# The MLP's first product as a seven-product step over channel pairs, with its result kept in DRAM

## The chip, the cores and the metric

The kernel runs on one core of a Trainium2 chip. A core has five engines that run their own instruction streams side by side and meet at semaphores: TensorE (PE in the profile, with its weight loads as PEld), VectorE (DVE), ScalarE (ACT), GpSimd (POOL) and SyncE (SP), which here issues nearly all DMA transfers, in the order of its stream. The time is that of the device for one execution, in microseconds (us); the median of several executions counts, and less is better.

## The reference, cut to what matters

The program computes two transformer-like blocks on 1024 tokens of width 1024: one with a recurrent mixer and a mixture of experts, then one with attention and an MLP. Only the end of the second block is touched:

```python
def second_block(x, c, ...):                     # cut to its last lines
    x = x + g_m * y                              # y: the attention's output product
    h = rms_norm_2(x, norm_mlp[i]) * (1 + sc_f) + sh_f
    x = x + g_f * (jnp.square(jax.nn.relu(h @ w_mlp_in[i])) @ w_mlp_out[i])
    return x                                     # h: 1024 x 1024, w_mlp_in: 1024 x 4096, w_mlp_out: 4096 x 1024
```

All is float32. The kernel splits each operand of a product into a high and a low part (both in the type fp32r) and adds three products: high by high, low by high, high by low.

## The kernel before, in words

The attention's output product (tiles "op", weights owh and owl, operand oyh and oyl) is made for eight tiles x2 of 128 tokens each. For the last four, tt = 4 to 7, the loop "for tt in range(4, 8)" issues per tile the loads of x (line 2152), a multiplication by fg on POOL (2153), the products, and the sum on DVE (1276, 2154). Between them stand the norms: net.norm_tiles makes xn from x2 (ACT line 820, DVE 84 to 97 and 823), and to_hT transposes xn on PE (834) and writes the operand of the MLP, h3h and h3l, split (ACT 836 and 841, DVE 839 and 842). There are 8 channel blocks k of 128, and two token halves of 512: half 0 is in place before the MLP starts, half 1 is made by last_half() in its midst.

The MLP (_mlp) runs over eight chunks c of 512 inner rows. phase_a(c) makes the first product: for each of four blocks u of 128 inner rows it loads 128 columns of w_mlp_in (line 74, tile ur), splits them into uh and ul (helper split: ACT line 66, DVE line 67), and for both token halves accumulates 8 x 3 matmuls of 128x128 by 512 columns in PSUM (proj_unit, mm3, lines 854 to 856, tile pj). Then ACT takes the relu (1592), DVE squares (1593), and a split writes mh and ml. phase_b(c) makes the second product: it loads and splits four blocks of w_mlp_out (w2h, w2l), and for each of eight token tiles accumulates 2 x 12 matmuls (tile mo); DVE multiplies by the gate (1633) and adds to x2 (1634). Chunk after chunk, the two phases alternate; in the last chunk x2 goes out (1636). In names such as pj<-h3h,uh the moving operand stands first and the stationary one second.

No list sets the order here: a scheduler orders each engine's stream, by the program's order and by when it reckons the operands to be there. Pools are stacks in SBUF, one growing from the left and one from the right (side=R).

Of the kernel before, what the change touches and what calls it, by code (L numbers as in the profile page):

```python
# [13 lines left out]
ALU = mybir.AluOpType  # L14
# [1561 lines left out]
def _mlp(self, wp, bp, ps, hT, w1, w2, x2, gate_row, out, last_half, first):

    nc = self.nc
    v = nc.vector
    gb = bp.tile([P, D], F32, name="mgb")  # L1580
    nc.sync.dma_start(gb, gate_row.to_broadcast([P, D]))
    NF = 8

    def phase_a(c):
        mids = [[bp.tile([P, S], F32R, name=n, bufs=5) for n in ("mh", "ml")] for u in range(4)]

        def piece(w, u, half):
            mh, ml = mids[u]
            sl = slice(half * 512, (half + 1) * 512)
            pt = self.proj_unit(ps, w, hT, half)  # L1590
            r = bp.tile([P, 512], F32, name="mr", bufs=2)
            nc.scalar.activation(r, pt, AF.Relu)  # L1592
            v.tensor_mul(r, r, pt)  # L1593
            self.split(mh[:, sl], ml[:, sl], r)

        def weight(u):
            f0 = c * 512 + u * P
            return self.wunit(wp, w1[:, f0:f0 + P])

        if c == 0:  # L1600
            for half in range(2):
                if half:
                    pools.extend(last_half())
                for u in range(4):
                    piece(first if (u, half) == (0, 0) else weight(u), u, half)
        else:
            for u in range(4):
                w = weight(u)
                for half in range(2):
                    piece(w, u, half)  # L1610
        return mids

    pools = []

    def phase_b(c, mids):
        W = []
        w2p = pools[0]
        for u in range(4):
            f0 = c * 512 + u * P
            raw = wp.tile([P, KC, P], F32, name="ur", bufs=2).rearrange("p k n -> p (k n)")  # L1620
            W.append(self.load_split(w2p, lambda r: [(r, w2[f0:f0 + P, :])], [P, D], "w2", 4, raw=raw))
        for tt in range(TT):
            sl = slice(tt * P, (tt + 1) * P)
            pts = [pools[1].tile([P, 512], F32, name="mo", bufs=4) for _ in range(2)]
            for u in range(4):
                for n in range(2):
                    cc = slice(n * 512, (n + 1) * 512)
                    self.mm3(pts[n], mids[u][0][:, sl], mids[u][1][:, sl], W[u][0][:, cc], W[u][1][:, cc],
                             u == 0, u == 3)
            for n in range(2):  # L1630
                cc = slice(n * 512, (n + 1) * 512)
                t = bp.tile([P, 512], F32, name="mt", bufs=1)
                v.tensor_mul(t, pts[n], gb[:, cc])  # L1633
                v.tensor_add(x2[tt][:, cc], x2[tt][:, cc], t)
            if c == NF - 1:
                nc.sync.dma_start(out[sl, :], x2[tt])
# [21 lines left out]
def program(net, ctx, I, out, dbg):  # L1658
# [35 lines left out]
    def each(t):  # L1694
        return [t[:, k:k + 1] for k in range(KC)]
# [442 lines left out]
        cf.close()  # L2138
    with ExitStack() as cx:
        xa = net.pool(cx, "x2a", side=R)  # L2140
        x2 = [xa.tile([P, D], F32, name=f"x2_{tt}") for tt in range(4)]
        co = ExitStack()
        ops = net.pool(co, "op_ps", space=PSUM, side="right")
        fg = net.pool(co, "fg2", side=R).tile([P, D], F32, name="fg2")
        nc.sync.dma_start(fg, final_g)
        op = OutProj(net, co, oTd, I["fox_w_out_2"][0], modd[1][2:3, :], ops, 2, x2, R, rd)

        def units(tts):
            for tt, n in tts:
# [51 lines left out]
        def norms(half):
            xns = []
            for i in range(4):
                tt = half * 4 + i
                xn = np_.tile([P, D], F32, name="xn", bufs=4)
                net.norm_tiles(np_, x2[tt], xn, rs[:, 0, tt:tt + 1], xn)
                xns.append(xn)
            return net.to_hT(np_, nps, 4 * half, xns, each(sc3), each(sh3), hT)
# [16 lines left out]
        wp = net.pool(cx, "ml_w", side=R)
        ps = net.pool(cx, "ml_ps", space=PSUM, side="right")

        def last_half():
            norms(1)
            cn.close()  # L2230
            return net.pool(cx, "ml_w2"), net.pool(cx, "ml_ps2", space=PSUM)

        net.mlp(wp, bp, ps, hT, I["w_mlp_in_2"][0], I["w_mlp_out_2"][0], x2, modd[1][5:6, :], out, last_half, first)
# [20 lines left out]
```

## Time and profile before

| what | us |
|---|---|
| median of 3 runs | 2637.94 |
| lowest and highest run | 2636.4 and 2642.43 |
| the profiled execution: its own time | 2636.1 |
| the profiled execution: its span | 2634.3 |

The span is what the profiler shows, from the first to the last instruction; the time holds a little more. Shares and stretches below are of the profiled execution. Starts are counted in us from the span's start. Matmul durations overlap, since one enters the array while the one before leaves it: a matmul of 512 columns is shown with about 0.39 us though the next starts after 0.23 us. The rate is therefore read from starts, or from a count of weight loads in a stretch.

### The profile page before, as it was taken

Reading aid. Unit: us, or ns where it says so; the run is one execution under the profiler, and the core shown is the slowest. Engines: PE = TensorE matmul, PEld = TensorE weight load, DVE = VectorE, ACT = ScalarE, POOL = GpSimd, SP = SyncE. Lnnn points to the kernel's source line nnn. Section 1 sums busy time; section 2 is a strip of 40 time slices with the busy share of each in tenths; the row PEclk is TensorE's granted clock in tenths of the full one; section 3 lists DMA queues with packets and bytes.
Section 4 is the critical chain, followed back from the end, with each engine's and each line's share of the span. In section 5 each row is a group of like instructions: output and inputs, shape, how many; then the busy total and the mean of one; then the engine's idle time right before and its main releaser. Section 6 shows DMA issues by size and latency. Waiting matters only on the chain.

```text
span 2634.3 us, 34681 instructions
## 1 busy us (share of the span) xinstructions
PE 2430.7 (92%) x11981; PEld 1950.9 (74%) x11981; DVE 1889.7 (72%) x3472; ACT 1335.8 (51%) x2435; POOL 424.9 (16%) x451
## 2 busy tenths in 40 slices
PE   6899989949999999986999999989999999999999
PEld 5677667737776666544898999977778888888887
DVE  7879886887979888986777887776654454444444
ACT  5556563246867767775677777763342122112210
POOL 2212110042314343531000000114100000000000
PEclk9999998969999999997999999999999999999999
DMA  8455564869999999983012111136141022112201
GB/s 268 126 148 177 160 219 146 272 246 299 369 346 367 338 358 326 367 310 114 28 49 49 48 47 47 36 90 189 46 122 48 17 64 64 35 30 64 64 28 69
DMA packets 243886, 407.86 MB, mean 155 GB/s; under 512 B 20432, under 2 KB 100164, under 8 KB 243708
## 3 DMA queue, kind: packets, MB, share of 16 engines
q1 hardware_dynamic: 235556, 386.70, 43.9%
q0 software_dynamic: 8032, 18.89, 3.2%
q8 instruction: 95, 1.56, 0.2%
q14 instruction: 83, 0.68, 0.1%
q10 hardware_dynamic: 120, 0.03, 0.0%
HBM read 376.74 MB, written 35.86 MB: 157 GB/s over the span
## 4 chain that ended last, share of the span: by engine, by line
PE 71%; DVE 14%; ACT 6%; DMA 4%; issue 4%; POOL 1%; SPq 0%; DVEq 0%; ACTq 0%; POOLq 0%
PE pj L854 8%; PE pj L855 8%; PE pj L856 8%; PE mo L854 5%; PE mo L856 5%; PE mo L855 5%; PE po L1513 2%; DVE wl L67 2%; PE op L856 2%; PE op L855 2%; PE op L854 2%; DVE aacc L782 2%; PE pT L1524 2%; PE pt L534 1%; PE pu L500 1%
## 5 line engine op out<-in xcount | busy, mean ns | idle before, releaser
L1592 ACT ACTIVATE mr<-pj 128x512 f32<-128x512 f32 x64 | 38.3, 598 | 497.2 <-PE pj L856 497.2
L67 DVE TENSOR_TENSOR wl<-wr,wh 128x1024 fp32r<-128x1024 f32 x210 | 249.8, 1229 | 28.8 <-ACT wh L66 27.7
L66 ACT ACTIVATE wh<-wr 128x1024 fp32r<-128x1024 f32 x216 | 220.5, 1054 | 86.7 <-PE po L464 30.9
L67 DVE TENSOR_TENSOR wl<-x,wh 128x1024 fp32r<-128x1024 f32 x164 | 192.4, 1217 | 26.3 <-ACT wh L66 25.6
L1633 DVE TENSOR_TENSOR mt<-mo,mgb 128x512 f32<-128x512 f32 x128 | 88.5, 692 | 163.6 <-PE mo L856 157.0
L854 PE MATMUL mo<-w2h,mh 128*128 128x512 f32 x512 | 202.5, 396 | 0.0
L855 PE MATMUL mo<-w2h,ml 128*128 128x512 f32 x512 | 202.5, 396 | 0.0
L856 PE MATMUL mo<-w2l,mh 128*128 128x512 f32 x512 | 202.5, 396 | 0.0
L854 PE MATMUL pj<-h3h,uh 128*128 128x512 f32 x504 | 198.7, 394 | 2.4 <-issue 2.4
L855 PE MATMUL pj<-h3h,ul 128*128 128x512 f32 x504 | 199.1, 395 | 0.9 <-DVE ul L67 0.9
L856 PE MATMUL pj<-h3l,uh 128*128 128x512 f32 x504 | 198.3, 394 | 0.0
L66 ACT ACTIVATE wh<-x 128x1024 fp32r<-128x1024 f32 x168 | 172.7, 1058 | 41.7 <-issue 9.1
L591 POOL DMA_INDIRECT x1d<-y,gidx x56 | 152.7, 2727 | 238.7 <-DMA x1d<-y,gidx 102.2
L854 PE MATMUL pj<-xh,h2h 128*128 128x384 f32 (+1 forms) x512 | 190.3, 372 | 0.8 <-DVE V L1433 0.7
L855 PE MATMUL pj<-xh,h2l 128*128 128x384 f32 (+1 forms) x512 | 176.0, 344 | 0.0
L856 PE MATMUL pj<-xl,h2h 128*128 128x384 f32 (+1 forms) x512 | 174.7, 342 | 0.0
L1593 DVE TENSOR_TENSOR mr<-mr,pj 128x512 f32<-128x512 f32 x64 | 44.0, 687 | 161.3 <-ACT mr L1592 161.3
L782 DVE SCALAR_TENSOR_TENSOR aacc<-aw,cs,aacc 128x512 f32<-128x512 f32 x160 | 131.1, 822 | 26.0 <-DMA aw<-in_w_ada 13.8
L67 DVE TENSOR_TENSOR pl<-pT,ph 128x512 fp32r<-128x512 f32 (+1 forms) x160 | 100.8, 634 | 25.0 <-ACT ph L66 21.5
L1501 ACT ACTIVATE Sx<-Sx,mx 128x128 f32<-128x128 f32 (+7 forms) x128 | 99.0, 773 | 38.3 <-DVE mx L1496 37.8
L856 PEld LDWEIGHTS mo<-w2l,mh 128*128 128x128 f32 x512 | 96.2, 188 | 23.3
L854 PEld LDWEIGHTS mo<-w2h,mh 128*128 128x128 f32 x512 | 96.2, 188 | 23.3
(525 smaller groups left out, 6591.5 us busy)
## 6 DMA issues: line engine op xcount, KB each, us to landing
wr<-in_w_expert_down SPq DMA_DIRECT2D x43, 1024.0 KB
wr<-in_w_expert_up SPq DMA_DIRECT2D x33, 1024.0 KB
x<-in_w_expert_gate SPq DMA_DIRECT2D x32, 1024.0 KB
wr<-in_w_expert_gate SPq DMA_DIRECT2D x32, 1024.0 KB
x<-in_w_expert_up SPq DMA_DIRECT2D x31, 1024.0 KB
aw<-in_w_ada SPq DMA_DIRECT2D x48, 512.0 KB
x<-in_w_expert_down SPq DMA_DIRECT2D x21, 1024.0 KB
aw<-in_ada_w SPq DMA_DIRECT2D x40, 512.0 KB
```

What stands on the lines that cost most here:

```text
L66: self.nc.scalar.activation(hi, src, AF.Copy)
L67: (v or self.nc.vector).tensor_sub(lo, src, hi.bitcast(F32))
L591: nc.gpsimd.indirect_dma_start(out=m.xd, out_offset=bass.IndirectOffsetOnAxis(ap=gi[0:r], axis=0), in_=y[o:o + r], in_offset=None, bounds_ ...
L782: nc.vector.scalar_tensor_tensor(acc, t[:, r, :], ccol[:, q:q + 1], acc, op0=ALU.mult, op1=ALU.add)
L854: nc.tensor.matmul(pt, sh, mh, start=first, stop=False)
L855: nc.tensor.matmul(pt, sl, mh, start=False, stop=False)
L856: nc.tensor.matmul(pt, sh, ml, start=False, stop=last)
L1501: nc.scalar.activation(Sx[:, 0:wd], Sx[:, 0:wd], AF.Exp, bias=mx[:, m - 1:m], scale=-1.0, accum_out=sm[:, q:q + 1])
L1513: nc.tensor.matmul(oc, vv, tiles[n][2 + t][:, at[r]:at[r] + 256], start=(kb + r == 0 and t == 0), stop=(kb + r == 2 * j + 1 and t == 1))
L1524: nc.tensor.transpose(pp[:, at[r] + q * P:at[r] + (q + 1) * P], Pj[q][:, (kb + r) * P:(kb + r + 1) * P], net.ident)
L1593: v.tensor_mul(r, r, pt)
L1633: v.tensor_mul(t, pts[n], gb[:, cc])
```

## The change

Two blocks of 128 inner rows, n's pair, are made together, and the contraction over 1024 channels is cut into two halves of 512 (k = 0 to 3 and 4 to 7). With the two token halves this gives a 2 by 2 by 2 block product, which a Strassen step (in Winograd's form) does with seven products of 4 x 3 matmuls instead of eight. The class Mlp holds the numbers o = 0 to 6 of the products. Their moving operands hc0 to hc6 are made once: hc0 and hc1 are the two channel halves of token half 0, hc2 to hc6 are token half 1 and sums and differences, made by half1(kk) in four steps between the first products. The stationary operands wc are made per pair from raw columns of w_mlp_in (rings of six raw tiles wr and four wc): prep adds or subtracts on POOL (lines 1648, 1650, 1651, 1656), then splits. step(g) calls prep(g + 3), issues product g's 12 matmuls and sums the results on DVE (1687 to 1702). inner takes relu and square in one DVE instruction (1707) and stores 512 columns to DRAM (rD). All 16 pairs are finished before the second product starts; that one loads the inner rows back ("m") with w_mlp_out ("w"), splits both (item) into the space of hc0 to hc6, and runs as before (block). The first four tiles of x2 go to DRAM and come back at g = 20, since half1 uses their space. PE's stream in the MLP is now fixed by hand.

```diff
-    for c in range(NF):
-        phase_b(c, phase_a(c))
+class Mlp:
+    NP = 16
+    LOOK = 3
...
+        duo = lambda a, os: [(n, o) for o in os for n in (a, a + 1)]
+        self.order = [(0, 0), (0, 1), (1, 0), (1, 1), (2, 0), (2, 1), (3, 0), (3, 1)]
+        self.todo = [("p", n) for n in range(4)]
+        for a in range(0, self.NP, 2):
+            self.order += duo(a, (3, 2, 4, 5, 6) if a < 4 else (0, 1, 3, 2, 4, 5, 6))
+            self.todo += [(k, a + i) for k in ("fg" if a else "gf") for i in range(2)]
+        self.todo += [(k, c, u) for c in range(8) for u in range(4) for k in "mw"]
...
+    def prep(self, g):
...
+        if o == 0:
+            src = A11
+        elif o == 1:
+            src = A12
+        elif o == 3:
+            src = self.S1[n] = self.pool.tile([P, 512], F32, name="hTt", bufs=2).rearrange("p (k n) -> p k n", k=4)
+            gp.tensor_add(src, A21, A22)
+        elif o == 2:
+            gp.tensor_sub(A21, A11, A21)
+            gp.tensor_sub(A11, self.S1.pop(n), A11)
+            src = A11
+        elif o == 4:
+            src = A21
+        elif o == 5:
+            gp.tensor_sub(A12, A12, A11)
+            src = A12
         else:
...
+            src = A22
+        wc = self.wc[g] = self.early.pop(0) if self.early else self.wp.tile([P, 2, 4, P], F32R, name="wc", bufs=4)
+        self.net.split(wc[:, 0], wc[:, 1], src)
...
+    def step(self, g):
...
+        self.prep(g + self.LOOK)
...
+        wc, h = self.wc.pop(g), self.hc[o]
+        for k in range(4):
+            net.mm3(pt, wc[:, 0, k, :], wc[:, 1, k, :], h[:, k, 0, :], h[:, k, 1, :], k == 0, k == 3)
+        if o == 0:
+            s = self.s[n] = self.wp.tile([P, 512], F32, name="s", bufs=4)
+            nc.scalar.activation(s, pt, AF.Copy)
...
+        elif o == 4:
+            s = self.s[n]
+            u = self.u[n] = self.wp.tile([P, 512], F32, name="c", bufs=4)
+            r = self.wp.tile([P, 512], F32, name="c", bufs=4)
+            v.tensor_add(u, s, pt)
+            z = self.Z.pop(n)
+            v.tensor_add(r, u, z)
+            v.tensor_add(s, s, z)
+            self.inner(r, n, 1, 1)
...
+    def inner(self, s, n, i, m):
+
+        self.net.nc.vector.scalar_tensor_tensor(s, s, 0.0, s, op0=ALU.max, op1=ALU.mult)
+        self.net.nc.sync.dma_start(self.rD[n][i][:, HALF[m]], s)
...
+        flat = [self.hc[o].rearrange("p k a n -> p (k a n)") for o in (0, 1, 3, 2, 4, 5, 6)]
+        self.slots = [t[:, i * 2048:(i + 1) * 2048].rearrange("p (a n) -> p a n", a=2) for t in flat for i in range(2)]
+        self.items = [(k, c, u) for c in range(8) for u in range(4) for k in "mw"]
...
+        hc = {o: xb.tile([P, 4, 2, 512], F32R, name=f"hc{o}") for o in range(2)}
...
+        hp = net.pool(cx, "hT3b", side=R)
+        for o in range(2, 7):
+            hc[o] = hp.tile([P, 4, 2, 512], F32R, name=f"hc{o}")
...
+            v.tensor_sub(T, t12, h[0][:, 0, :].bitcast(F32))
+            v.tensor_sub(T, T, h[0][:, 1, :].bitcast(F32))
+            net.split(h[3][:, 0, :], h[3][:, 1, :], T)
+            nc.gpsimd.tensor_sub(t12, t22, t12)
+            nc.gpsimd.tensor_sub(T, t22, T)
+            net.split(h[5][:, 0, :], h[5][:, 1, :], t22)
+            net.split(h[2][:, 0, :], h[2][:, 1, :], T)
+            net.split(h[4][:, 0, :], h[4][:, 1, :], t12)
+            nc.gpsimd.tensor_sub(t22, h[1][:, 0, :].bitcast(F32), T)
+            v.tensor_add(t22, t22, h[1][:, 1, :].bitcast(F32))
+            net.split(h[6][:, 0, :], h[6][:, 1, :], t22)
+
+        with tc.manual_schedule(engines={mybir.EngineType.PE}):
+            for g in range(len(mlp.order)):
+                if g in range(2, 6):
+                    half1(g - 2)
...
+                mlp.step(g)
```

Two places show how the streams move. The first is POOL at the start of the MLP. Before, its last work is the multiplication of x2's tiles 6 and 7 by fg, and the branch at the program's end follows:

```order
L2153 TENSOR_TENSOR x2_4_19574<-x2_4_19574,fg2_18831 128x1024 [waits DMAHW5_49,DVE_49]
L2153 TENSOR_TENSOR x2_5_19575<-x2_5_19575,fg2_18831 128x1024 [waits DMAHW6_49,DVE_49]
L2153 TENSOR_TENSOR x2_6_19576<-x2_6_19576,fg2_18831 128x1024 [waits DMAHW7_49,DVE_49]
L2153 TENSOR_TENSOR x2_7_19577<-x2_7_19577,fg2_18831 128x1024 [waits DMAHW0_49,DVE_49]
L1653 UNCONDITIONAL_BRANCH
```

Now, from half1's last step on (2363, 2364 and 2368 are its three POOL lines; wr_20354 and wr_20356 are the raw tiles "g" of pairs 0 and 1, wr_20358 and wr_20360 their "f", hTt_20370 and hTt_20392 the sums for product 3):

```order
L2363 TENSOR_TENSOR x2a_18854<-x2a_18854 128x512 [waits DVE_49]
L1648 TENSOR_TENSOR hTt_20370<-wr_20354 128x512 [waits DMAHW1_49,DVE_49,Pool_49]
L1650 TENSOR_TENSOR wr_20354<-wr_20358,wr_20354 128x512 [waits DMAHW5_49,DMAHW7_49,DMAHW3_49,Pool_49]
L1651 TENSOR_TENSOR wr_20358<-hTt_20370,wr_20358 128x512 [waits PE_49,Pool_49]
L1656 TENSOR_TENSOR wr_20358<-wr_20358 128x512 [waits Pool_49]
L2364 TENSOR_TENSOR hTt_20337<-x2a_18854,hTt_20337 128x512 [waits DVE_49]
L2368 TENSOR_TENSOR x2a_18854<-hc1_19613,hTt_20337 128x512 [waits Pool_49]
L1648 TENSOR_TENSOR hTt_20392<-wr_20356 128x512 [waits DMAHW4_49,DVE_49]
L1650 TENSOR_TENSOR wr_20356<-wr_20360,wr_20356 128x512 [waits DMAHW7_49,Pool_49]
L1651 TENSOR_TENSOR wr_20360<-hTt_20392,wr_20360 128x512 [waits PE_49,Pool_49]
```

Four POOL instructions for pair 0 now stand between the first and the second of half1's last step, and pair 1's sum behind both; nine more of half1 stand ahead.

The second place is DVE at the same time. Before, while half 1 of h3 is made (h3l1_2 to h3l1_5 are its low parts, mr the inner rows, ml their low parts, ul a weight's low part):

```order
L1593 TENSOR_TENSOR mr_20211<-mr_20211,pj_20186 128x512 [waits Activation_49]
L842 TENSOR_TENSOR h3l1_2_20048<-hTt_20295,h3h1_2_20047 128x512 [waits Activation_49]
L67 TENSOR_TENSOR ml_20077<-mr_20211,mh_20076 128x512 [waits Activation_49]
L839 CAST h3h1_3_20049<-hTt_20304 128x512 [waits Activation_49]
L842 TENSOR_TENSOR h3l1_3_20050<-hTt_20304,h3h1_3_20049 128x512 [waits DVE_49]
L842 TENSOR_TENSOR h3l1_4_20052<-hTt_20313,h3h1_4_20051 128x512 [waits Activation_49]
L839 CAST h3h1_5_20053<-hTt_20322 128x512 [waits Activation_49]
L842 TENSOR_TENSOR h3l1_5_20054<-hTt_20322,h3h1_5_20053 128x512 [waits DVE_49]
L67 TENSOR_TENSOR ul_20391<-ur_20388,uh_20390 128x1024 [waits DMAHW7_49,PE_49,Activation_49]
```

Now, the end of the same work (wc_20372, wc_20394, wc_20414 and wc_20436 are the stationary operands of steps 8 to 11, hTt_20337 and x2a the temporaries of half1's last step):

```order
L67 TENSOR_TENSOR hc3_20133<-hTt_20337,hc3_20133 128x512 [waits Activation_49]
L67 TENSOR_TENSOR wc_20372<-hTt_20370,wc_20372 128x512 [waits PE_49,Pool_49]
L1687 TENSOR_TENSOR c_20388<-s_20323,X_20375 128x512 [waits PE_49]
L67 TENSOR_TENSOR hc2_20132<-hTt_20337,hc2_20132 128x512 [waits Activation_49]
L2369 TENSOR_TENSOR x2a_18854<-x2a_18854,hc1_19613 128x512 [waits Pool_49]
L1707 SCALAR_TENSOR_TENSOR c_20388<-c_20388 128x512 [waits DVE_49]
L67 TENSOR_TENSOR wc_20394<-hTt_20392,wc_20394 128x512 [waits Activation_49]
L67 TENSOR_TENSOR hc6_20136<-x2a_18854,hc6_20136 128x512 [waits Activation_49]
L67 TENSOR_TENSOR wc_20414<-wr_20358,wc_20414 128x512 [waits DMAHW5_49,PE_49]
L1687 TENSOR_TENSOR c_20430<-s_20410,X_20417 128x512 [waits PE_49]
L67 TENSOR_TENSOR wc_20436<-wr_20360,wc_20436 128x512 [waits DMAHW7_49,Activation_49]
```

From half1's first subtraction (line 2360) to the last of these rows DVE now has 43 instructions of 128x512, of which three read PSUM (line 1687) and 40 read two operands from SBUF.

## Rows read from the trace of the kernel before

**Rows 1.** The page: busy time by engine, and the chain by engine.

```profile
PE 2430.7 (92%) x11981; PEld 1950.9 (74%) x11981; DVE 1889.7 (72%) x3472; ACT 1335.8 (51%) x2435; POOL 424.9 (16%) x451
...
PE 71%; DVE 14%; ACT 6%; DMA 4%; issue 4%; POOL 1%; SPq 0%; DVEq 0%; ACTq 0%; POOLq 0%
```

**Rows 2.** Stretches of the MLP: length, busy by engine (count), clock, DMA.

```profile
core 0: us, PE busy (x) PEld busy (x) DVE busy (x) ACT busy (x) POOL busy (x), PEclk, DMA share, GB/s
1959.90:2004.70 44.80, 44.80 (x193) 36.07 (x192) 24.99 (x35) 4.26 (x5) 0.00 (x0) 1.00 0.17 49
2004.70:2048.97 44.27, 44.27 (x194) 36.05 (x192) 19.95 (x25) 14.95 (x21) 0.00 (x0) 1.00 0.27 84
...
2628.20:2634.30 6.10, 0.13 (x1) 0.00 (x0) 2.23 (x4) 0.00 (x0) 0.00 (x0) 0.90 0.21 86
```

**Rows 3.** Two pieces of one first-product chunk: half 0, then half 1.

```profile
2004.70:2010.30 5.60, 5.60 (x25) 4.51 (x24) 2.27 (x4) 0.00 (x0) 0.00 (x0) 1.00 0.00 0
2010.30:2015.77 5.47, 5.47 (x26) 4.51 (x24) 1.38 (x2) 1.23 (x2) 0.00 (x0) 1.00 0.01 3
```

**Rows 4.** Matmuls by tile: ns min/median/max, first and last start.

```profile
L854 PE MATMUL mo<-w2h,mh x512: 395/396/397, 1959.9 to 2627.5; 128*128 128x512 f32 x171
...
L854 PE MATMUL pj<-h3h,uh x504: 389/395/628, 1915.0 to 2582.7; 128*128 128x512 f32 x168
...
L854 PE MATMUL pj<-h1h,uh x256: 387/389/793, 44.2 to 354.2; 128*128 128x512 f32 x128
```

**Rows 5.** Groups of lines, the attention's output product, 1880 to 1905.

```profile
L854 PE MATMUL op<-owh,oyh 128*128 128x512 f32 x38 | 14.8, 389 | 0.0
```

**Rows 6.** The MLP's start, by stretches.

```profile
1905.50:1912.50 7.00, 6.78 (x33) 5.26 (x31) 2.98 (x8) 1.64 (x5) 0.00 (x0) 1.00 0.52 153
1912.50:1915.00 2.50, 0.10 (x1) 0.01 (x1) 0.73 (x2) 1.65 (x3) 0.00 (x0) 1.00 0.82 202
1915.00:1920.00 5.00, 4.24 (x11) 3.18 (x12) 4.71 (x6) 3.51 (x5) 0.00 (x0) 0.66 0.42 118
```

**Rows 7.** The chain of waits there: start, length, what.

```profile
1907.63 6.21 DMA ur<-in_w_mlp_in
```

**Rows 8.** ACT in order of time, same place.

```profile
1907.28 1.06 ACT L820 ACTIVATE xn<-x 128x1024 f32<-128x1024 f32 x1 [9.07 <-DVE x L2154]
...
1914.83 0.61 ACT L66 ACTIVATE mh<-mr 128x512 fp32r<-128x512 f32 x1
...
1916.51 0.76 ACT L836 ACTIVATE hTt<-hTp,cols,sc 128x512 f32<-128x512 f32 x1
```

**Rows 9.** POOL in order of time, 1777 to 1790.

```profile
1778.01 1.69 POOL L1260 TENSOR_TENSOR x<-x,rb 128x512 f32<-128x512 f32 x1 [1.68 <-DMA rb<-rd]
1782.23 1.28 POOL L1260 TENSOR_TENSOR x<-x,rb 128x512 f32<-128x512 f32 x1 [2.53 <-DMA rb<-rd]
...
1786.90 1.63 POOL L1260 TENSOR_TENSOR x<-x,rb 128x512 f32<-128x512 f32 x1
```

**Rows 10.** DVE in order of time, beside those POOL instructions.

```profile
1777.89 0.69 DVE L67 TENSOR_TENSOR oyl<-x,oyh 128x512 fp32r<-128x512 f32 x1
1778.49 1.75 DVE L67 TENSOR_TENSOR owl<-x,owh 128x512 fp32r<-128x512 f32 x1
...
1786.69 0.68 DVE L67 TENSOR_TENSOR owl<-x,owh 128x512 fp32r<-128x512 f32 x1
1787.29 0.68 DVE L67 TENSOR_TENSOR pl<-pT,ph 128x512 fp32r<-128x512 f32 x1
1787.89 0.68 DVE L1496 CUSTOM_DVE_ANT_0 Sx<-Fb,pS 128x512 f32<-128x512 f32 x1
```

**Rows 11.** POOL's groups with shapes apart, whole span.

```profile
L2153 POOL TENSOR_TENSOR x<-x,fg 128x1024 f32<-128x1024 f32 x8 | 19.4, 2441 | 23.3 <-DVE rs_t L96 15.0 <-DVE x L2154 3.9 <-DMA x<-x1d 3.8
L1260 POOL TENSOR_TENSOR x<-x,rb 128x512 f32<-128x512 f32 x14 | 19.0, 1360 | 26.2 <-DMA rb<-rd 24.9 <-DVE x L2154 1.3
```

**Rows 12.** DVE's groups with shapes apart, 1950 to 2600.

```profile
L1634 DVE TENSOR_TENSOR x<-x,mt 128x512 f32<-128x512 f32 x116 | 80.2, 691 | 4.0
...
L67 DVE TENSOR_TENSOR w2l<-ur,w2h 128x1024 fp32r<-128x1024 f32 x32 | 39.2, 1224 | 10.5 <-ACT w2h L66 10.4
```

More of the change, by code (lines that the diff above doesn't have):

```diff
@@ L1573, in attend @@
         return front, back, gates
[L1576 to L1605, printed above, removed]
-        else:
[L1607 to L1621, printed above, removed]
@@ L1622, in phase_b @@
         for tt in range(TT):
             sl = slice(tt * P, (tt + 1) * P)
-            pts = [pools[1].tile([P, 512], F32, name="mo", bufs=4) for _ in range(2)]
+            pts = [self.px.tile([P, 512], F32, name="X", bufs=6) for _ in range(2)]
             for u in range(4):
+                m, w = self.op["m", c, u], self.op["w", c, u]
                 for n in range(2):
-                    cc = slice(n * 512, (n + 1) * 512)
-                    self.mm3(pts[n], mids[u][0][:, sl], mids[u][1][:, sl], W[u][0][:, cc], W[u][1][:, cc],
-                             u == 0, u == 3)
+                    net.mm3(pts[n], m[:, 0, sl], m[:, 1, sl], w[:, 0, HALF[n]], w[:, 1, HALF[n]], u == 0, u == 3)
+                if tt == TT - 1 and u == 0:
+                    for _ in range(2):
+                        self.item()
@@ L1630, in phase_b @@
             for n in range(2):
[L1631 to L1636, printed above, removed]
-    for c in range(NF):
-        phase_b(c, phase_a(c))
-Net.mlp = _mlp
+                cc = HALF[n]
+                t = self.wp.tile([P, 512], F32, name="s", bufs=4)
@@ L1645 @@
+                v.tensor_mul(t, pts[n], self.gb[:, cc])
+                v.tensor_add(self.x2[tt][:, cc], self.x2[tt][:, cc], t)
+            if c == 7:
+                nc.sync.dma_start(self.out[sl, :], self.x2[tt])
+            if tt < 6 and self.at < 8 * c + 14:
+                self.item()
 _INS = ["x", "c", "ada_w", "ada_b", "norm1_g", "w_in", "conv_w", "conv_b", "w_q", "w_k", "b_igate", "b_fgate",
@@ L1679, in program @@
     x1d = scratch("x1d", [S, D])
+    x2d = scratch("x2d", [512, D])
+    rD = [[scratch(f"rD{n}_{i}", [P, S]) for i in range(2)] for n in range(Mlp.NP)]
     oTd = [scratch(f"oTd{i}", [D, 512]) for i in range(2)]
@@ L2140, in program @@
         xa = net.pool(cx, "x2a", side=R)
-        x2 = [xa.tile([P, D], F32, name=f"x2_{tt}") for tt in range(4)]
+        x2a = xa.tile([P, 4, D], F32, name="x2a")
+        x2 = [x2a[:, tt, :] for tt in range(4)]
         co = ExitStack()
@@ L2194, in program, with norm @@
         x2 += [xb.tile([P, D], F32, name=f"x2_{tt}") for tt in range(4, 8)]
+        hc = {o: xb.tile([P, 4, 2, 512], F32R, name=f"hc{o}") for o in range(2)}
         hT = HT()
-        hT.alloc(0, xb, "h3")
+        hT.t[0] = [tuple(hc[k // 4][:, k % 4, a, :] for a in range(2)) for k in range(KC)]
+        np_ = net.pool(cx, "n4")
         cn = ExitStack()
-        np_ = net.pool(cn, "n4")
         nps = net.pool(cn, "n4_ps", space=PSUM)
[L2201 to L2208, printed above, removed]
+        mlp = Mlp(net, np_, hc, I["w_mlp_in_2"][0], I["w_mlp_out_2"][0], rD)
+        mlp.early = []
+        def norm(tt, t):
+            xn = t.rearrange("p k n -> p (k n)")
+            net.norm_tiles(np_, x2[tt], xn, rs[:, 0, tt:tt + 1], xn)
+            return xn
         for k in range(KC):
@@ L2225, in program @@
[L2225 to L2233, printed above, removed]
+                xns = [mlp.slot(("x", i)) for i in range(4)]
+                last = net.to_hT(np_, nps, 0, [norm(i, xns[i]) for i in range(4)], each(sc3), each(sh3), hT)
@@ new lines, in program @@
+                mlp.loads(2)
+                for i in range(4):
+                    mlp.done(("x", i))
+                xns = [mlp.slot(("x", i)) for i in range(4, 8)]
+            xns[tt - 4] = norm(tt, xns[tt - 4])
+        co.close()
+        mlp.wp = net.pool(cx, "ml_w", side=R)
+        for g in range(Mlp.LOOK):
+            mlp.prep(g)
+        hp = net.pool(cx, "hT3b", side=R)
+        for o in range(2, 7):
+            hc[o] = hp.tile([P, 4, 2, 512], F32R, name=f"hc{o}")
+        mlp.px = net.pool(cx, "ml_ps", space=PSUM, side=R)
@@ new lines, in program, with half1 @@
+        tmp = x2a.rearrange("p t (a n) -> p (t a) n", a=2)
+        def half1(kk):
+            t12, t22 = tmp[:, kk, :], tmp[:, 4 + kk, :]
+            for k, t in ((kk, t12), (kk + 4, t22)):
+                pt = nps.tile([P, 512], F32, name="hTp", bufs=2)
+                for i, xn in enumerate(xns):
+                    nc.tensor.transpose(pt[:, i * P:(i + 1) * P], xn[:, k * P:(k + 1) * P], net.ident)
+                nc.scalar.activation(t, pt, AF.Identity, scale=sc3[:, k:k + 1], bias=sh3[:, k:k + 1])
+            T = np_.tile([P, 512], F32, name="hTt", bufs=2)
+            h = [hc[o][:, kk] for o in range(7)]
+            v.tensor_sub(T, t12, h[0][:, 0, :].bitcast(F32))
[9 more added lines that the diff above has]
+            net.split(h[6][:, 0, :], h[6][:, 1, :], t22)
@@ new lines, in program @@
+        with tc.manual_schedule(engines={mybir.EngineType.PE}):
+            for g in range(len(mlp.order)):
+                if g in range(2, 6):
+                    half1(g - 2)
+                    if g == 5:
+                        for i in range(4, 8):
+                            mlp.done(("x", i))
+                        mlp.loads()
+                        cn.close()
+                        mlp.pz = net.pool(cx, "ml_z", space=PSUM)
+                mlp.step(g)
+                if g == 20:
+                    for tt in range(4):
+                        nc.sync.dma_start(x2[tt], x2d[tt * P:(tt + 1) * P, :])
+                if g == len(mlp.order) - 6:
+                    mlp.open_second(x2, modd[1][5:6, :], out)
+                if g >= len(mlp.order) - 6:
+                    mlp.item()
+            for _ in range(2):
+                mlp.item()
+            for c in range(8):
+                mlp.block(c)
```

96 lines of the change are left out of this document (88 added, 8 removed).

## The prediction, made before the changed kernel ran

> **What bounds the kernel now.** I began with the page's busy line and its chain by engine: TensorE is busy for 92% of the span and holds 71% of the chain, so the reader should look for the time in PE's stream first [rows 1]. Next I cut the MLP into its stretches. [...] By the stretches the first product runs at 44.27 / 192 = 0.2306 us per matmul, the second at 44.80 / 192 = 0.2333.
>
> Within a chunk of the first product the two halves differ: 24 matmuls on token half 0 take 5.60 us (0.2333 each), 24 on half 1 take 5.47 (0.228) [rows 3]. The durations by tile say the same: all of the second product at 396 ns, the first between 389 and 395, products of the early stages with h1h at 389 [rows 4], the attention's output product at 389 [rows 5]. So there are two rates. Going by the durations, the faster one is 0.2333 - 0.0065 = 0.2268 us.
>
> [...] After the last matmul stands a tail of 6.10 us [rows 2].
>
> **What the change removes.** A pair of blocks takes 7 products of 12 matmuls each where it took 8 times 12: 16 x 7 x 12 = 1344 instead of 1536. The 192 that go are worth 192 x 0.2306 = 44.3 us, all of it on the path. The second product keeps its 1536.
>
> **The rate of those that stay.** In the built program I compared where, in bytes of a partition modulo 128, the moving and the stationary tile begin. Where the rows show 389 ns the two agree (op: 96 and 96; half 1 of h3: 96 and 96); where they show 395 or 396 they differ (half 0 of h3: 64 against 96; the second product: 64 against 96). In the changed program wc begins at 96, hc0 and hc1 at 64, hc2 to hc6 at 96; in the second product a pair m and w lies in one of the hc tiles, so both agree throughout. If this is the cause, and not only a coincidence of four cases, products 0 and 1 stay at 0.2333, the other five and the whole second product go at 0.2268. The bounds are 0.2268 and 0.2333 for all; I take the split by tiles, since it fits every row that I have.
>
> **What the start of the MLP gains in waits.** This is the largest cost. half1 and the first sums of prep put POOL instructions of 128x512 in the midst of DVE's, as the rows of the two orders show. The trace has such neighbours: while POOL runs a 128x512 operation from 1778.01 for 1.69 us, a DVE operation on two SBUF operands that was issued at 1778.49 takes 1.75 us instead of about 0.68 and ends after POOL does. One that reads PSUM, issued within a POOL operation (1786.90, 1.63 us), keeps its 0.68 [rows 9, 10]. So two operations of this kind don't overlap, and their times add up; if they overlapped, the stretch below would cost only the longer of its two sums, 24.7 us, and be over before step 12 is due (the second rival). [...]
>
> From half1's first subtraction to the low part of wc_20436, which step 11 waits for, DVE has 43 instructions, 40 of them on two SBUF operands. Back to back their starts are 0.60 us apart [rows 10]: 24.0 us. POOL has 19 in that stretch, which I put at 1.30 each (1.28 is the undisturbed one [rows 9], the mean of the group is 1.36 [rows 11]): 24.7 us. Together 48.7 us.
>
> It begins thus. xn of the last token tile ends on ACT at 1908.3 [rows 8], then the first weights are split, and step 0 starts near 1909.7. PE has been idle and the clock is low as it is now at this place, so steps 0 and 1 and the first transposes last until about 1918.6. With one eviction on ACT (0.76 us [rows 8]) the serial work starts at 1919.6 and can end at 1968.3; handovers between DVE, POOL and ACT leave gaps, 3.7 us by going through the order by hand, so 1972. Step 11 lasts 2.75 us and ends near 1975.3 with its handover. PE will have been idle for the most part ahead of step 8 (some 14 us) and step 9 (some 5 us), and works off its clock again: after 2.5 us of idling it lost 5 x 0.34 = 1.7 us [rows 6], here I put 2.5. Step 12 starts at 1977.8. Without the stall it would be 1918.6 + 10 x 2.75 + 3 x 1.0 for the transposes of half1's later steps = 1949.1. The stall costs about 29 us, with 0 (all of it overlaps) and 45 (POOL at 1.69 instead of 1.30, 19 x 0.39 = 7.4 more; gaps twice as long, 3.7 more; twice as much lost at the low clock and in later handovers, 5 more) as its bounds.
>
> **What lies beside PE afterwards.** Two pairs, 14 steps, give PE 168 matmuls: 168 x 0.228 = 38.3 us. DVE has 36 instructions of 128x512 in that time (14 splits, 14 sums, 8 of line 1707), at 0.62 us 22.3 us (0.691 at the most [rows 12]: 24.9), POOL 8 at 1.30, 10.4 us. Even all in series that is 32.7 us of 38.3, and preparation runs three steps (8.3 us) ahead. Without that cover each us above 38.3 would cost 8 us in all. Stores of the inner rows and loads of the weights use queues that stand at 0.27 at the most now [rows 2]. I take nothing for it. At the change to the second product DVE has the first 8 splits of 128x1024 (1.224 us each [rows 12]) and about 8 us ahead; 1 us. In a chunk of the second product DVE has 8 x 1.22 + 32 x 0.69 = 31.9 us beside 192 x 0.2268 = 43.5; nothing. Ahead of the MLP POOL still multiplies by fg, at 2.44 us each [rows 11], and tiles of x2 go out to DRAM and return; I see nothing that ends last there, and put 0, with 4 us to either side.
>
> **The sum.** 1977.8 + 288 x 0.2333 (67.2) + 912 x 0.2268 (206.8) + 1536 x 0.2268 (348.4) + 1 + 6.1 = 2607.3 us of span. The profiled execution's own time is 1.8 us over its span (2636.1 and 2634.3), and the median of the runs is 1.8 over that (2637.94): 2611 us.
>
> **The rivals.** (a) The place of the tiles doesn't set the rate. Then 1200 matmuls go at 0.2306 and 1536 at 0.2333, 276.7 + 358.4 = 635.1 instead of 622.4: 2624 us. For it speaks that four cases are few. [...] Chance 0.17.
>
> (b) The start is hidden: DVE and POOL overlap after all where their operands lie otherwise, and step 12 starts near 1952: 2611 - 26 = 2585 us. For it speaks that only a few neighbours of this kind are in the trace; against it, that a DVE operation that met one ran 1.1 us longer, just until after POOL's end [rows 9, 10]. Chance 0.13.
>
> (c) Slower: DVE and POOL in series pace the whole first product. POOL's group of line 2153 has 2441 ns for an instruction [rows 11], though of double width; if prep's subtractions cost that much among DVE's, and DVE's 0.69, a duo of pairs takes 8 x 2.44 + 36 x 0.69 = 44.4 us instead of 38.3. Eight times 6.1 is 49 us: 2660. It decides from about 2.1 us for one POOL instruction (27 us of gain / 8 = 3.4 us per duo). Against it, POOL's operations of 128x512 took 1.28 to 1.69. Chance 0.08.
>
> That the matmuls aren't saved is excluded: the order has 192 fewer.
>
> **How the numbers follow.** The forecast has 0.55, with its own range of 2600 to 2622; (a) 0.17, (b) 0.13, (c) 0.08; 0.07 is for a start or early part that costs more than reckoned, between 2622 and 2643. A measurement of this kernel can tell about 0.2%, 5.3 us, from no change: faster is below 2632.7, slower above 2643.2. Faster are the forecast, (a), (b) and a part of the rest: 0.87; the same 0.05; slower, (c), 0.08. The range from 2590 to 2633 leaves out most of (b) and (c).
>
> **What would show it.** In the profile after: PE's idle time ahead of products 2 of the first pairs, ended by DVE or POOL; DVE operations on two SBUF operands that last 1.3 to 1.8 us beside POOL's; later duos of about 38 us with PE busy throughout; matmuls with hc0 and hc1 at 395 ns, with hc2 to hc6 at 389; the second product's chunks at 43.5 us instead of 44.8. I am wrong if PE waits in later duos as well, if the second product still shows 396 ns, or if the MLP's start runs without stalls.

## The result and the profile after

The changed kernel takes 2611.22 us (median of 4 runs, 2609.64 to 2612.59) where the kernel before takes 2637.17 (4 runs): the ratio is 0.9898, with a 95% interval from 0.9881 to 0.9915. The profiled execution took 2609.64 us, its span is 2607.9. On the page, the busy line that answers to [rows 1]:

```profile
PE 2386.0 (91%) x11789; PEld 1920.5 (74%) x11789; DVE 2014.5 (77%) x3648; ACT 1346.6 (52%) x2447; POOL 551.4 (21%) x527
```

PE has 192 instructions fewer, and still 91% of the span. The stretches that answer to [rows 2, 3, 6] (length, busy time by engine with counts, granted clock, DMA share, GB/s):

```profile
1911.69:1919.37 7.68, 7.47 (x24) 5.71 (x25) 4.26 (x10) 2.77 (x6) 0.00 (x0) 0.78 0.49 138
1919.37:1930.60 11.23, 11.16 (x61) 9.09 (x59) 10.43 (x11) 7.37 (x12) 6.17 (x4) 1.00 0.24 70
1930.60:1946.40 15.80, 11.89 (x44) 9.35 (x44) 13.95 (x20) 9.52 (x16) 6.91 (x5) 0.78 0.62 171
1946.40:1970.82 24.42, 10.36 (x25) 7.15 (x25) 22.02 (x19) 6.41 (x11) 19.62 (x13) 0.65 0.33 96
...
2020.01:2031.22 11.21, 11.21 (x50) 9.02 (x49) 6.11 (x9) 3.50 (x6) 3.20 (x2) 1.00 0.13 48
2031.22:2058.44 27.22, 27.22 (x121) 22.52 (x120) 19.53 (x28) 6.36 (x10) 9.71 (x7) 1.00 0.43 135
2250.80:2294.85 44.05, 44.05 (x194) 36.03 (x192) 29.35 (x41) 5.78 (x7) 0.00 (x0) 1.00 0.30 101
2426.91:2470.46 43.55, 43.55 (x194) 36.05 (x192) 29.25 (x41) 7.89 (x9) 0.00 (x0) 1.00 0.29 97
2601.80:2607.90 6.10, 0.45 (x2) 0.02 (x1) 2.38 (x4) 0.00 (x0) 0.00 (x0) 0.80 0.21 86
```

The first four rows are the MLP's start, where PE works for 10.36 of the last 24.42 us, at a mean clock of 0.65. The next two are one duo of pairs: four steps with hc0 and hc1 (48 matmuls, 0.2335 us each), then ten with hc2 to hc6 (120, 0.2268 each), PE busy throughout. Two chunks of the second product follow, of 44.05 and 43.55 us, against 44.80 before.

What PE waits for between 1900 and 2260 (waiting instruction, releaser: us in total, times, longest):

```profile
PE Z L854 <- ACT wc L66: 7.3, 1, 7.3
PE Z L855 <- DVE wc L67: 6.8, 2, 4.1
PE hTp L2356 <- ACT x2a L2357: 4.0, 2, 3.3
PE X L854 <- ACT rs_y L91: 3.4, 1, 3.4
PE X L855 <- DVE wc L67: 0.2, 1, 0.2
```

All of it lies ahead of 1967; for the rest of the span the view lists no wait of PE. The products "Z" that wait are steps 8 and 9, product 3 of the first two pairs. What DVE and POOL do just then, each in order of time:

```profile
1951.93 3.42 DVE L67 TENSOR_TENSOR hc<-x2a,hc 128x512 fp32r<-128x512 f32 x2
1955.27 1.75 DVE L67 TENSOR_TENSOR hc<-hTt,hc 128x512 fp32r<-128x512 f32 x1
1956.94 1.74 DVE L67 TENSOR_TENSOR wc<-hTt,wc 128x512 fp32r<-128x512 f32 x1
1958.61 0.68 DVE L1687 TENSOR_TENSOR c<-s,X 128x512 f32<-128x512 f32 x1
```

```profile
1951.54 1.59 POOL L1648 TENSOR_TENSOR hTt<-wr 128x512 f32<-128x512 f32 x1 [1.28 <-issue]
1953.21 1.60 POOL L1650 TENSOR_TENSOR wr<-wr 128x512 f32<-128x512 f32 x1
1954.88 1.59 POOL L1651 TENSOR_TENSOR wr<-hTt,wr 128x512 f32<-128x512 f32 x1
1956.55 1.59 POOL L1656 TENSOR_TENSOR wr<-wr 128x512 f32<-128x512 f32 x1
1958.10 1.73 POOL L2364 TENSOR_TENSOR hTt<-x2a,hTt 128x512 f32<-128x512 f32 x1
```

They take turns, one instruction each, nearly all of them 1.67 us apart. The DVE operation at 1958.61, which reads PSUM, runs its 0.68 us in the midst of a POOL operation, as in [rows 10].

### The profile page after: what moved, and what is told of

Same layout as the page of the kernel before. It is cut to its first block, busy times and chain, and to the rows that moved or that the text cites. A ratio compares the mean times of both kernels' runs of the same rounds, so it can differ in the third digit from the quotient of the medians.

```text
span 2607.9 us, 34881 instructions
## 1 busy us (share of the span) xinstructions
PE 2386.0 (91%) x11789; PEld 1920.5 (74%) x11789; DVE 2014.5 (77%) x3648; ACT 1346.6 (52%) x2447; POOL 551.4 (21%) x527
## 3 DMA queue, kind: packets, MB, share of 16 engines
q1 hardware_dynamic: 250532, 424.45, 48.8%
## 5 line engine op out<-in xcount | busy, mean ns | idle before, releaser
L67 DVE TENSOR_TENSOR wl<-x,wh 128x1024 fp32r<-128x1024 f32 x164 | 192.6, 1219 | 26.8 <-ACT wh L66 25.4
L66 ACT ACTIVATE hc<-wr 128x1024 fp32r<-128x1024 f32 x64 | 64.6, 1056 | 266.8 <-PE X L855 244.8
L856 PE MATMUL X<-hc 128*128 128x512 f32 x512 | 200.3, 391 | 0.0
L854 PE MATMUL X<-hc 128*128 128x512 f32 x512 | 200.3, 391 | 0.0
L855 PE MATMUL X<-hc 128*128 128x512 f32 x512 | 199.7, 390 | 0.0
L1748 DVE TENSOR_TENSOR s<-X,mgb 128x512 f32<-128x512 f32 x128 | 86.5, 690 | 123.2 <-PE X L856 123.1
L854 PE MATMUL X<-hc,wc 128*128 128x512 f32 x384 | 151.9, 396 | 3.4 <-ACT rs_y L91 3.4
L855 PE MATMUL X<-hc,wc 128*128 128x512 f32 x384 | 151.7, 395 | 0.2 <-DVE wc L67 0.2
L856 PE MATMUL X<-hc,wc 128*128 128x512 f32 x384 | 151.4, 394 | 0.0
L66 ACT ACTIVATE wc<-wr 128x512 fp32r<-128x512 f32 x96 | 60.5, 633 | 166.6 <-PE X L856 118.7
L855 PEld LDWEIGHTS X<-hc 128*128 128x128 f32 x512 | 96.1, 188 | 21.2
L856 PEld LDWEIGHTS X<-hc 128*128 128x128 f32 x512 | 96.1, 188 | 21.1
```

Source lines behind the costliest of these rows:

```text
L66: self.nc.scalar.activation(hi, src, AF.Copy)
L67: (v or self.nc.vector).tensor_sub(lo, src, hi.bitcast(F32))
L854: nc.tensor.matmul(pt, sh, mh, start=first, stop=False)
L855: nc.tensor.matmul(pt, sl, mh, start=False, stop=False)
L856: nc.tensor.matmul(pt, sh, ml, start=False, stop=last)
L1748: v.tensor_mul(t, pts[n], self.gb[:, cc])
```

## The experiments

In the profiles of the changed kernel and of those made from it the MLP's first matmul starts between 1906.5 and 1919.7, in those of the kernel before and of the two made from that one between 1903.2 and 1906.5, though the edits below concern what comes later. Where two profiles are set against each other, stretches are therefore counted from that matmul; the medians are given beside it.

**The count alone.** The kernel before, without one of the eight channel blocks in its first product:

```diff
-            pt = self.proj_unit(ps, w, hT, half)
+            pt = self.proj_unit(ps, w, hT, half, kc=KC - 1)
```

> The kernel before, with the channel block k = 7 left out of the MLP's first product: 192 of its 1536 matmuls go (the result is then that of seven of eight channel blocks), and nothing else changes. It measures what the count alone is worth. Theory (PE bounds the MLP, the time is matmuls by rate): 192 x 0.2306 = 44.3 us less, about 2594. Rival (with fewer matmuls DVE, ACT or the weight loads end last in the chunks, so that part of the 44 us is not gained): 2600 to 2615.

Measured: 2594.03 us against 2637.18 for the kernel before (ratio 0.9827, interval 0.9808 to 0.9847), 43.2 us less. The first chunk of the kernel before, then the first chunk, the first of the second product and the next one of the first product in this kernel, and the longest wait of PE in the second of these:

```profile
1906.55:1959.90 53.35, 49.92 (x218) 39.66 (x219) 29.86 (x43) 27.34 (x40) 0.00 (x0) 0.97 0.40 118
```

```profile
1903.18:1952.61 49.43, 45.65 (x194) 35.93 (x195) 28.93 (x42) 27.00 (x40) 0.00 (x0) 0.93 0.39 117
1952.61:1998.96 46.35, 45.33 (x193) 35.91 (x192) 25.88 (x35) 4.84 (x6) 0.00 (x0) 1.00 0.20 57
1998.96:2037.62 38.66, 38.66 (x169) 31.55 (x168) 19.97 (x25) 15.15 (x21) 0.00 (x0) 1.00 0.31 96
```

```profile
PE mo L854 <- ACT w2h L66: 0.7, 1, 0.7
```

From the first matmul to the end the two profiles differ by 41.6 us (727.8 and 686.2). Each of the seven later chunks gives 44.27 - 38.66 = 5.6 us, 24 matmuls at 0.2333, with PE busy throughout: there the count is worth what the rate says, and nothing else ends last. At the start it isn't paid in full: the first chunk gives 3.9, and the first one of the second product becomes 1.5 us longer, since PE now waits there for splits. The change as a whole gave 26 us.

**The place of the tiles, in the changed kernel.** hc0 and hc1 moved to agree with the rest:

```diff
+        xb.tile([P, 8], F32, name="shift")
         hc = {o: xb.tile([P, 4, 2, 512], F32R, name=f"hc{o}") for o in range(2)}
```

> The tiles hc0 and hc1 begin 32 bytes later in a partition, so that they too stand at 96 modulo 128 as wc and hc2 to hc6 do. Theory (a matmul costs 0.2267 us where moving and stationary tile, and those of its neighbours, agree in their place modulo 128 and 0.2333 where they differ): products 0 and 1 go at 0.2267 like the rest, 384 x 0.0066 = 2.5 us less, of which some 2 outside the stalled start; the second product loses its mixture (0.2287 on average now) and goes at 0.2267 throughout, 1536 x 0.002 = 3 us less. Together 5 us, about 2606. Rival (products 0 and 1 are slow for another reason, as their place in the order or what DVE and ACT do beside them): 0.2333 stays for them, no change.

Measured: 2604.55 us (ratio 0.9861, 0.9842 to 0.9879), 6.7 below the changed kernel. The stretches of this kernel from step 0 to step 12, to the second product, to the end, and four steps with hc0 and hc1:

```profile
1913.46:1978.25 64.79, 46.37 (x177) 35.91 (x177) 53.37 (x61) 27.45 (x47) 32.70 (x20) 0.79 0.39 114
1978.25:2250.25 272.00, 272.00 (x1202) 225.22 (x1200) 195.28 (x269) 79.26 (x121) 90.72 (x56) 1.00 0.42 133
2250.25:2604.20 353.95, 348.32 (x1537) 288.10 (x1535) 226.90 (x316) 51.75 (x52) 0.00 (x0) 1.00 0.26 90
2021.80:2032.68 10.88, 10.88 (x50) 9.01 (x49) 6.23 (x9) 3.50 (x6) 3.23 (x2) 1.00 0.13 49
```

The same in the changed kernel:

```profile
1911.69:1976.49 64.80, 46.56 (x176) 35.98 (x177) 53.39 (x61) 27.34 (x47) 32.70 (x20) 0.79 0.39 114
1976.49:2250.80 274.31, 274.31 (x1201) 225.20 (x1200) 195.10 (x269) 79.80 (x122) 90.34 (x56) 1.00 0.42 132
2250.80:2607.90 357.10, 351.45 (x1537) 288.17 (x1535) 227.71 (x316) 51.31 (x52) 0.00 (x0) 1.00 0.26 89
```

The start stays (64.8), 1200 matmuls take 272.00 us instead of 274.31 (0.2267 each, those with hc0 and hc1 too), and the second product with its tail 353.95 instead of 357.10. Together 5.5 us, by the stretches, as the theory had it.

**The same from the other side**: hc2 to hc6 moved away from wc.

```diff
         for o in range(2, 7):
             hc[o] = hp.tile([P, 4, 2, 512], F32R, name=f"hc{o}")
+        hp.tile([P, 8], F32, name="shift")
```

> The tiles hc2 to hc6 begin 32 bytes earlier, at 64 modulo 128, where hc0 and hc1 stand; wc stays at 96. Theory (agreement of moving and stationary decides): in the first product every moving tile now differs from wc, so all products go at 0.2333: 104 later steps, of which some 72 were fast, 72 x 12 x 0.0066 = 5.7 us more there. In the second product all operands stand at 64 and agree, so it goes at 0.2267 throughout, 1536 x 0.002 = 3 us less. Time about 2614. Rival (a tile at 64 is slow in itself, whatever its partner): the second product slows too, to 0.2333 throughout, 2611 + 5.7 + 7 = 2624. Rival (the place has no part in it): 2611 with the same pattern as before, products 0 and 1 alone slow.

Measured: 2609.83 us (ratio 0.9885, 0.9868 to 0.9903); its profiled execution began the MLP 8 us later than the changed kernel's. The stretches as above, and its matmuls by tile (ns min/median/max):

```profile
1984.66:2264.66 280.00, 280.00 (x1201) 225.41 (x1200) 194.48 (x272) 81.33 (x123) 90.33 (x56) 1.00 0.41 132
2264.66:2618.70 354.04, 348.35 (x1537) 288.10 (x1535) 225.08 (x313) 50.17 (x51) 0.00 (x0) 1.00 0.25 88
```

```profile
L854 PE MATMUL X<-hc x512: 387/389/389, 2264.7 to 2612.2; 128*128 128x512 f32 x171
L854 PE MATMUL X<-hc,wc x384: 389/396/775, 1919.7 to 2264.0; 128*128 128x512 f32 x192
```

The whole first product now goes at 280.00 / 1200 = 0.2333, 396 ns, and the whole second one at the faster rate, 389 ns, with every tile of it at 64. So a tile at 64 is not slow in itself: it is the agreement of moving and stationary that counts. By the stretches this kernel is 5.7 - 3.1 = 2.6 us slower than the changed one; the medians (1.4 us the other way) can't tell so little.

**The same edit in the kernel before**, which has nothing of the seven products:

```diff
+        xb.tile([P, 8], F32, name="shift")
         hT.alloc(0, xb, "h3")
```

> The kernel before, with one edit: half 0 of h3 begins 32 bytes later, and with it the tiles w2h and w2l of the second product, so that both stand at 96 modulo 128 like their partners uh and mh. Theory (placement decides the rate): half 0's 768 matmuls and the second product's 1536 go at 0.2267 instead of 0.2333, 2304 x 0.0066 = 15.2 us less, about 2622 instead of 2637. Rival (the rates of before have another reason): no change, 2637.

Measured: 2621.34 us against 2638.27 (ratio 0.9929, 0.9912 to 0.9946), 16.9 less; by the stretches from the first matmul it is 14.9 (727.8 and 712.9), where the theory had 15.2. So 32 bytes of empty space are worth more than half of what the change gave. The rows that answer to [rows 4]:

```profile
L854 PE MATMUL mo<-w2h,mh x512: 389/389/389, 1958.3 to 2610.5; 128*128 128x512 f32 x171
...
L854 PE MATMUL pj<-h3h,uh x504: 389/389/765, 1912.8 to 2566.9; 128*128 128x512 f32 x168
```

**The sums at the start, on DVE instead of POOL.**

```diff
-        gp = self.net.nc.gpsimd
+        gp = self.net.nc.vector
...
-            nc.gpsimd.tensor_sub(t12, t22, t12)
-            nc.gpsimd.tensor_sub(T, t22, T)
+            v.tensor_sub(t12, t22, t12)
+            v.tensor_sub(T, t22, T)
...
-            nc.gpsimd.tensor_sub(t22, h[1][:, 0, :].bitcast(F32), T)
+            v.tensor_sub(t22, h[1][:, 0, :].bitcast(F32), T)
```

> All subtractions and additions that half1 and prep issue on POOL are issued on DVE instead; nothing else changes. Theory (POOL and DVE operations on two SBUF operands exclude each other, so their times add up at the MLP's start): 19 POOL operations of 1.30 us or more leave the serial work and 19 DVE operations of 0.60 us (11.4 us) enter it, 48.7 us become 35.4. The start-up stall shrinks by about 13 us: step 12 starts near 1963 to 1965 instead of 1976.5, and the time is about 2598 us. Rival (the two engines overlap and DVE alone is the bound at the start): DVE gets 11.4 us more, step 12 starts near 1988, the time is about 2622. Second rival (the start waits for evictions on ACT or for weights, not for these sums): no change, 2611. Later stages: DVE has 44 instead of 36 instructions per duo of pairs, 27 of 38 us, no cost by either.

Measured: 2595.64 us (ratio 0.9829, 0.9812 to 0.9846), 15.6 below the changed kernel. Its stretches from step 0 to step 12 and on to the second product, and what PE waits for from 1900 to 1970:

```profile
1914.12:1965.65 51.53, 44.04 (x176) 33.61 (x177) 47.25 (x81) 27.24 (x47) 0.00 (x0) 0.87 0.50 143
1965.65:2239.74 274.09, 274.09 (x1201) 225.33 (x1200) 209.61 (x328) 80.26 (x122) 0.00 (x0) 1.00 0.42 134
```

```profile
PE X L855 <- DVE wc L67: 5.0, 3, 4.2
PE X L854 <- ACT rs_y L91: 3.4, 1, 3.4
PE Z L855 <- DVE wc L67: 1.5, 2, 1.2
PE Z L854 <- ACT wc L66: 1.0, 1, 1.0
```

The start is 64.80 - 51.53 = 13.3 us shorter, although DVE now has 20 instructions more (81 instead of 61 in the stretch). Had the two engines overlapped, it would have become longer. That it is just the 13.3 of 48.7 - 35.4 is in part luck: a POOL instruction in turn with DVE's added 1.67 - 0.60 = 1.07 us, not 1.30, so the exchange itself is worth 20 x 0.47 = 9.4 us. PE's waits after the first two matmuls fall from 18.0 us to 7.3; the other 2.6 go with the higher granted clock (0.87 instead of 0.79 over the stretch). Its DVE busy time even fell, from 53.39 to 47.25 us: the long rows before (up to 1.78 us for one instruction) held waiting; from 1920 on each now takes 0.68 to 0.71 us. The rest goes at the rate it had.

**Both edits together**, the diff of hc0 and hc1 and that of the sums.

> The changed kernel with both edits: all sums on DVE, and hc0 and hc1 32 bytes later. Theory: the two gains are at different places and add up, 2611 - 13.5 - 5.5 = 2592 us. Rival (they share something, so that the second gain is smaller): 2595 to 2598.

Measured: 2588.51 us (ratio 0.9817, 0.9794 to 0.984).

```profile
1906.49:1957.96 51.47, 43.79 (x176) 33.60 (x177) 47.23 (x81) 27.30 (x47) 0.00 (x0) 0.87 0.48 143
1957.96:2229.96 272.00, 272.00 (x1201) 225.30 (x1200) 209.32 (x328) 80.30 (x122) 0.00 (x0) 1.00 0.43 135
2229.96:2583.90 353.94, 348.32 (x1537) 288.20 (x1535) 225.14 (x313) 50.67 (x51) 0.00 (x0) 1.00 0.26 89
```

The start has the one gain (51.47), the two products have the other (272.00 and 353.94): from step 0 it is 696.2 - 677.4 = 18.8 us shorter than the changed kernel, 13.3 and 5.5. They add up.

**What is left of the stall.** half1 in three parts, in the kernel with both edits (half1 makes T and hc3, half1b hc4 and hc2, half1c hc5 and hc6):

```diff
                 if g in range(2, 6):
                     half1(g - 2)
...
+                if g in (6, 7):
+                    half1b(2 * g - 12)
+                    half1b(2 * g - 11)
+                if g in (10, 11):
+                    half1c(2 * g - 20)
+                    half1c(2 * g - 19)
                 mlp.step(g)
```

> As the kernel with both edits, and half1 is made in three parts: T and hc3 between steps 2 and 5 as before, hc4 and hc2 issued at steps 6 and 7, hc5 and hc6 at steps 10 and 11, with 4 DVE operations more than before (T is not kept). Theory (what is left of the stall is DVE's queue: hc6 and hc5 are made ahead of the operands of steps 8 to 11, which wait behind them): step 8 no longer waits, step 10 waits some 3 to 5 us, the MLP's start gets 8 to 9 us shorter, about 2583. Rival (the rest of the stall is latency from engine to engine, not the amount of work in the queue): within 2 us of the kernel with both edits.

Measured: 2587.15 us (ratio 0.9801, 0.9779 to 0.9822), 1.4 us below the kernel with both edits, which the medians can't tell from nothing. Its stretches from step 0 to step 12, to step 16, to the second product, and PE's waits from 1900 to 1975:

```profile
1911.29:1956.65 45.36, 40.63 (x176) 32.54 (x177) 41.70 (x72) 25.01 (x43) 0.00 (x0) 0.92 0.41 116
1956.65:1969.52 12.87, 11.78 (x49) 8.86 (x48) 12.69 (x22) 4.20 (x7) 0.00 (x0) 1.00 0.74 228
1969.52:2231.75 262.23, 262.23 (x1154) 215.91 (x1152) 204.25 (x321) 78.04 (x119) 0.00 (x0) 1.00 0.43 137
```

```profile
PE X L854 <- ACT wc L66: 3.9, 2, 3.7
PE X L854 <- ACT rs_y L91: 3.4, 1, 3.4
PE X L855 <- DVE wc L67: 1.9, 5, 0.6
```

Step 8 no longer waits, step 10 now waits 3.7 us, as expected, and step 12 comes 6.1 us earlier (45.36 against 51.47). But steps 12 to 15, which take 48 x 0.2267 = 10.9 us elsewhere, take 12.87 here with DVE busy for 12.69 of them, another 1.1 us goes in the steps behind (262.23 for 1152 x 0.2267 = 261.1), and from step 0 to the end the gain is 677.4 - 674.4 = 3.0 us. I had expected 8 to 9. That the waits moved with the work, and that DVE is busy where PE then falls behind, speaks for the theory that DVE's queue is what is left: deferring work takes none of it away, it adds four instructions, and DVE had no idle time up to step 16 to put them into. The time itself lies where the rival had it (within 2 us by the medians), so the size failed, and a share of latency from engine to engine is not excluded.

## Why the prediction was right, step by step

The forecast was 2611, its span 2607.3; measured 2611.22 and 2607.9. That is closer than its terms: they were off by up to 3.3 us, and the errors cancelled, so that it met the time within 0.3 us is luck.

- **The removed matmuls** (44.3 us): right where the pipeline runs, 5.6 us a chunk: there PE was busy before for all of the 44.27 us, at a granted clock of 1.00 [rows 2]. Alone, start included, they are worth 43.2 by the medians and 41.6 by the stretches.
- **The rate of those that stay, first product** (1200 matmuls, 274.0 us): right, 274.31, with products 0 and 1 at 0.2333 and the rest at 0.2268, as the split by tiles had it. That place causes it is shown by moving tiles one way (272.00 us for the 1200), the other way (280.00), and in the kernel before (14.9 us less). Rival (a), that it doesn't, is out.
- **The rate of the second product** (348.4 us): wrong by 2.9, the largest miss that added time. The step that failed is "a pair m and w lies in one of the hc tiles, so both agree throughout". They do, and yet every chunk with an operand in hc0 or hc1 took about 44.05 us; only the two without any, the fifth and the seventh, took 43.55. Bringing all tiles to one place, 96 or 64, gave the faster rate to all (348.3). So it isn't enough that a matmul's own operands agree: the ones next to it count. The starts show where: in the first chunk 12 of the 24 matmuls of each token tile have their operands in hc0 and hc1, and only the last matmul before a change of place and the five to seven behind it take 224 to 236 ns from start to start (means of the token tiles by place); the others take 226.6 to 226.8, at 64 as at 96. A chunk with 6 such matmuls of 24 has as many changes and takes as long. A change of place of the stationary tiles isn't needed for it: in a duo they stand at 96 throughout, and the first five matmuls behind products 0 and 1 still take 228 to 236 ns. The cause stays open.
- **The start** (step 0 to step 12, 1909.7 to 1977.8, 68.1 us): right in its mechanism, 64.80 measured, and out of the same causes only in part. Step 0 came 2.0 us later than I put it, since xn on ACT came later. The serial work from half1's first subtraction (1921.46) to the low part of wc_20436 (1970.28) took 48.8 us: my sum was 48.7, and 52.4 with gaps. In 47.8 of these 48.8 us DVE or POOL ran something, so the two in series are what the stretch is made of. In the sum errors cancel: a pair of instructions in turn takes 1.67 us, not 0.60 + 1.30 = 1.90, and the gaps, with both engines idle, were 1.0 us instead of 3.7, but I had left out DVE's three instructions on PSUM, and a twentieth of POOL fell into the stretch (1966.31). By the measured prices it is 43 x 0.60 + 20 x 1.07 + 1.0 = 48.2. The last wait was not the one I named: step 9 waited for its own low part until 1966.84, and step 11 for nothing.
- **PE's idle time and clock.** I put 14 us of idling ahead of step 8 and 5 ahead of step 9. It was 7.3 ahead of step 8, 4.1 within it, 2.7 within step 9, and 4.0 earlier, where half1's transposes wait for an eviction that stands behind splits in ACT's stream; that wait I had not seen. The clock cost more than the 2.5 us that I put (before, 2.5 us of idling were followed by 5 us at a mean clock of 0.66 [rows 6]): of the stretch of 24.42 us, 14.05 are waits and 25 x 0.2267 = 5.7 the matmuls at full clock, so some 4.7 went to the granted clock, 0.65 on average there (from 1959.33 to 1963.17 the matmuls come 0.427 us apart).
- **Beside PE afterwards**: right. A duo takes 11.21 + 27.22 = 38.43 us (38.3), with DVE at 25.6 and POOL at 12.9 us, their waits for each other included (one of them or both are busy in 26.8 us of it), and PE waits for nothing. Rival (c), that they pace the first product, is out: POOL's instructions cost 1.3 to 1.8 us, under the 2.1 at which it would have decided.
- **Rival (b)**, a hidden start, is out by the waits (18.0 us of PE behind the first two matmuls), and its premise by the sums on DVE (a start shorter by 13.3 us).
- **The change to the second product** (1 us): about 0.2. **The tail** (6.1): 5.8.

The balance, by the two profiles: 44.3 us less by the count and 2.4 + 7.1 less by the rates (276.7 to 274.3, 358.4 to 351.3). Against that the start costs more. Before, the first chunk took 53.35 us, 9.1 over its 192 matmuls at 0.2306; now the first 144 matmuls take 64.80, 31.6 over theirs: 22.5 more. And the MLP's first matmul comes 5.1 us later (1911.69 and 1906.55), about half of it since step 0 now stands behind the last xn on ACT; that this xn itself starts 2.6 us later (1909.92 and 1907.28) no run explains. Together 26.2 us less, and the two spans differ by 26.4.

## What to carry to other kernels

A saving on the busiest engine was paid out in full only where its operands were ready (without one channel block, 5.6 us in each later chunk of the first product and 3.9 in the first), so add up what the new operands cost on every engine at the place where the pipeline is still empty, and, for instructions on two SBUF operands, add DVE's and POOL's times there instead of taking the longer (the start's serial work took 48.8 us, where the longer of its two sums was 24.7). A slower instruction on an idle engine can cost more than the same work on a busy, faster one: moving POOL's sums to DVE shortened the start by 13.3 us. Where equal matmuls at an equal clock show two durations, look at where their tiles begin: 32 bytes were worth 14.9 us in one kernel and 5.5 in the other, by the stretches.

## What was not expected of the hardware

- Matmuls of 128x128 by 512 at full clock come every 0.2267 or every 0.2333 us, by the places of moving and stationary tiles modulo 128 bytes: 64 and 64, or 96 and 96, give the first; 64 and 96 the second. Another unlike pair stands in the kernel before, whose first matmuls have half 0 of h3 (64) as moving and u0h (0) as stationary tile:

```profile
L854 PE MATMUL pj<-h3h,u0h x8: 394/394/472, 1906.5 to 1911.5; 128*128 128x512 f32 x8
```

  They are slow too (from 1906.86 to 1911.99 they start 0.2332 us apart), though 0 and 64 agree modulo 64. Whether 128 is the number, or a multiple of it, no run shows. After a stretch of unlike operands a few like ones still go slowly: the first 12 matmuls with hc2 to hc6 in a duo took 0.2287 us on average, the next 12 took 0.2267 (from their starts). The slower rate stands in the second product before too, 44.80 us for 192 matmuls, where POOL ran nothing [rows 2], so it doesn't take POOL. That PE's rate hangs on where its operands lie these runs show, but not by what.
- A POOL and a DVE operation of 128x512, each on two SBUF operands, in turn take 1.67 us together, though alone the one took 1.28 us [rows 9] and the others start 0.60 apart [rows 10]: they exclude each other, but for 0.2 of 1.9 us.
